# Causal mask added on VectorE together with the row maximum; opening transfers merged and cut smaller; the first norm's ones product one unit later

## The chip, the cores and the metric

The kernel runs on one core of one Trainium2 chip. The metric is device time in microseconds of one execution: three executions of the kernel before took 1414.01, 1414.11 and 1414.16 us, median 1414.11. The profiled execution is a further one, with its own time. Engines are named as in the profile: PE is TensorE's matmul, PEld its weight load, DVE is VectorE, ACT is ScalarE, POOL is GpSimd, SP is SyncE (which only issues transfers here; SPq and ACTq are the issuing instructions of two DMA queues).

## The reference

A decoder trunk of two layers over 528 tokens (16 learned meta tokens and 512 real ones), width 1024, all float32. Layer 0 mixes with an mLSTM group (4 heads, chunked) and an RG-LRU group; layer 1 with differential attention, 8 heads of two 64-wide query/key halves each; each layer is followed by a squared-ReLU MLP, with an RMS norm ahead of every part. What the change touches is the first norm and projection of layer 0, and the softmax of layer 1:

```python
h = x*rsqrt(mean(x*x)+eps)*g ; proj = h @ w_in            # layer 0, first product of the program
...
s = einsum('bhcqd,bhckd->bhcqk', qb, kh)                  # layer 1, c = 0, 1
p = softmax(where(k_pos <= q_pos, s, -inf))
pd = p[:, :, 0] - lam * p[:, :, 1]
out = einsum('bhqk,bhkv->bhqv', pd, vh)
```

## The kernel before

Tokens lie along the free dimension (528 columns), features on the 128 partitions, so an activation of width 1024 is 8 tiles of 128x528. A float32 product is made of three passes with reduced-precision operands: each operand is split into a high part (ACT's cast) and a low part (DVE's subtraction, the helper at L162), and PE computes high*high, high*low and low*high. A weight "unit" is 128x1024: it feeds 8 blocks of 128 columns, so a unit on all 528 tokens is 8 x 3 x 2 = 48 matmuls of 264 columns (L425). SP loads each unit; ACT casts it (L240) and DVE subtracts (L162).

**The opening.** `OPENING` (L78) is the order of the first transfers: the halves A0, A1 of the first unit, B0, B1 of the second, the eight blocks x0 to x7 of the input, and `pk`, a packed table of 116 constants per partition with the norm's gains. Two of them (x0 and pk, marked *) go out on ACT's queue, the rest on SP's (L562 to L578). `norm_x` (L474) turns block k into its scaled high part (ACT, L480) and low part (DVE, L482); `ahead_of` splits the weight halves between them. `TURNS` (L79) is the order in which `two_units` (L430, matmuls at L439) takes blocks 0 to 7 of the two units A and B: 96 matmuls. Until the first data are there PE runs 16 matmuls on a tile of ones (`N_WARM`, L179). The scale of the norm, 1/sqrt(mean square), is applied later, to the products: ACT squares the eight blocks (L515), POOL adds them (L517), ACT and DVE split the sum, PE multiplies it with a matrix of ones (L531), and ACT and DVE form `rstd`.

**The order of work** of layer 0 is the table `PLAN` (L46): `q00 q02` are the two units of the opening, `S` the squares, `N` the ones product with what follows it, `q01 q03` two more units, `e` the gate unit, `c0` the first unit whose result is multiplied with `rstd`.

**The attention.** `attend(hd)` (L1120) computes the q, k and v units of one head; `attn_steps` gives the steps s0 to s3 (scores and softmax of one block of 128 queries), t0 to t3 (transposes of the probabilities), v, o and f (values, output product, norm). `SLOTS` (L31) says at which of six places between the matmuls of `attend` each step of the previous heads is put (a ' means one head further back), and the scheduler then merges them into one instruction order per engine. A score step (L1188) has per half c one or two spans of at most 400 columns, each in one of the four "ax" PSUM banks: two matmuls (L1203, L1205), and for the span that holds the diagonal a third one of an identity with a bfloat16 matrix that is -2^100 above the diagonal (L1202 or L1208; both operands lie in `keepb`). DVE takes the negated row maximum (L1210; with two spans one more operation, L1214), ACT computes exp(score - maximum) from PSUM with the row sum (L1217). Later L1226 and L1227 scale and subtract the two halves.

Of the kernel before, what the change touches and what calls it, by code (L numbers as in the profile page):

```python
# [30 lines left out]
SLOTS = ("t2' s0 t1'", '', "t3'", 's1', "o' t0 s2 v", "f' s3")  # L31
# [15 lines left out]
q00 q02 S q01 N q03 e c0 q04 A o0 G0 B g0 q12 m1 c1 K q05 q10 C G1 m1 p1 p1 g1 o1 p1 p1 R0 q11 m2  # L47
# [76 lines left out]
def trunk(tc, hT, wu, wri, pk, lv, rope, gf, out, probe=None):  # L124
# [7 lines left out]
    with ctx:  # L132
# [36 lines left out]
        keep = cp.tile([P, T], F32, name="keep")  # L169
        keepr = cp.tile([P, P], F32R, name="keepr")  # L170
        ones, ident, mkf, pkt = (keep[:, i * P:i * P + w] for i, w in enumerate((P, P, P, N_PK)))
        onesr = keepr[:, 0:P]
        keepb = cp.tile([P, 2 * P], mybir.dt.bfloat16, name="keepb")
        mkr, idr = (keepb[:, i * P:(i + 1) * P] for i in range(2))
        nc.vector.memset(onesr.bitcast(F32), 1.0)
        nc.vector.memset(ones, 1.0)
        warm = axt("warm")
        for _ in range(N_WARM):
            nc.tensor.matmul(warm[:, :2 * P], onesr, onesr[:, None, :].to_broadcast([P, 2, P]), start=True, stop=True)  # L179
        epsc = cp.tile([P, 1], F32, name="epsc")  # L180
# [293 lines left out]
        def norm_x(h, gc, lo, tag, late=False, hold=KB, then=None):  # L474

            x = [xt(f"{tag}x{k}") for k in range(KB)]
            fin = []
            for k in range(KB):
                hk = h[:, k, lo:]
                fin_x = nc.scalar.activation(out=x[k][0][:, lo:], in_=hk, func=AF.Copy, scale=pc(gc + k))  # L480
# [80 lines left out]
        last = {}  # L561
        for t in OPENING:  # L562
            if t == "##":
                with tc.issue_after(last[True].ins):
                    last[True] = nc.scalar.copy(cp.tile([P, 1], F32, name="first"), ones[:, 0:1])
                continue
            on = t.endswith("*")
            eng = nc.scalar if on else nc.sync
            with tc.issue_after(last[on].ins) if on in last else nullcontext():
                if t[:2] == "pk":  # L570
                    last[on] = eng.dma_start(out=pkt, in_=pk)
                elif t[0] == "x":
                    i = int(t[1])
                    last[on] = eng.dma_start(out=h0[:, i, :], in_=hT[:, i, :])
                else:
                    u, i = "AB".index(t[0]), int(t[1])
                    c = slice(i * HALF, (i + 1) * HALF)
                    last[on] = eng.dma_start(out=raws[u][:, c], in_=wu[seq[u]][:, c])  # L578

        c = slice(0, HALF)  # L580
        state["first"] = nc.vector.tensor_copy(out=ready[0][0][:, c], in_=raws[0][:, c])

        def ahead_of(k):
            seen = [t[:2] for t in OPENING if t[:2] not in ("pk", "##")]
            at = 0 if k == 0 and seen[0][0] != "x" else seen.index(f"x{k}") + 1
            while at < len(seen) and seen[at][0] != "x":
                u, i = "AB".index(seen[at][0]), int(seen[at][1:])
                c = slice(i * HALF, (i + 1) * HALF)
# [491 lines left out]
        for i in range(2):  # L1080
# [12 lines left out]
        nc.vector.memset(mkf, 0.0)  # L1093
        nc.gpsimd.affine_select(out=mkf, in_=mkf, pattern=[[-1, P]], compare_op=ALU.is_ge, fill=NEG, base=0,
                                channel_multiplier=1)
        nc.vector.tensor_copy(out=mkr, in_=mkf)
        nc.vector.tensor_copy(out=idr, in_=ident)
# [74 lines left out]
        def attn_steps(hd, rot, vr):  # L1172
# [15 lines left out]
            def sstep(I):  # L1188
# [5 lines left out]
                for c in range(2):  # L1194
# [4 lines left out]
                    for r, (d, s0, m) in list(enumerate(spans))[::-1 if c else 1]:  # L1199
                        masked = s0 + m == nk  # L1200
                        if c and masked:
                            nc.tensor.matmul(d[:, m - P:m], idr, mkr, start=True, stop=False, skip_group_check=True)  # L1202
                        nc.tensor.matmul(d[:, :m], qS[c][:, qs], kS[c][:, s0:s0 + m], start=not (c and masked),  # L1203
                                         stop=False, skip_group_check=True)
                        nc.tensor.matmul(d[:, :m], qS[c][:, qs], kL[c][:, s0:s0 + m], start=False,  # L1205
                                         stop=bool(c) or not masked, skip_group_check=True)
                        if not c and masked:
                            nc.tensor.matmul(d[:, m - P:m], idr, mkr, start=False, stop=True, skip_group_check=True)  # L1208
                        with pri("E"):
                            nc.vector.tensor_reduce(out=mx[:, 2 * c + r:2 * c + r + 1], in_=d[:, :m], axis=AX.X, op=ALU.max,  # L1210
                                                    negate=True)
                    with pri("E"):
                        if len(spans) == 2:
                            nc.vector.tensor_tensor(out=mx[:, 2 * c:2 * c + 1], in0=mx[:, 2 * c:2 * c + 1],  # L1214
                                                    in1=mx[:, 2 * c + 1:2 * c + 2], op=ALU.min)
                        for r, (d, s0, m) in enumerate(spans):
                            nc.scalar.activation(out=e[:, s0:s0 + m], in_=d[:, :m], func=AF.Exp,  # L1217
                                                 bias=mx[:, 2 * c:2 * c + 1], accum_out=ss[:, c + 2 * r:c + 2 * r + 1])
# [154 lines left out]
def lay_out(x, meta_tokens, norm_mix, norm_mlp, norm_final, ab_w_in, ab_if_bias, mlstm_norm, lru_conv_w, lru_conv_b,  # L1373
# [81 lines left out]
    return {"hT": hT, "wu": wu.reshape(N_UNIT, P, 1024), "wri": wri, "pk": pk, "lv": lv, "rope": rope,  # L1455
# [18 lines left out]
```

## Time and profile before

| what | value |
|---|---|
| time, median of 3 (range) | 1414.11 us (1414.01 to 1414.16) |
| time of the profiled execution | 1414.54 us |
| its span, first to last instruction | 1412.7 us |
| PE busy | 1399.7 us, 99% |
| DVE / ACT / POOL busy | 72% / 54% / 13% |
| mean clock granted to PE | 0.998 |

How to read it: an engine's busy time is counted in the span; what lies between the span and the time (1.8 us here) is start and end. Matmuls overlap in the record (each is shown from its start to its modelled end), so the price of one in a row of them is the distance to the next start, not its duration. A group of instructions is shown as line, engine, operation, output<-inputs, shape and count, then busy time, mean ns of one, and the idle time ahead of it with what ended it.

### The profile page before, as it was taken

What the parts mean: (1) busy time and instruction counts of PE and PEld (TensorE: products, weight loads), DVE (VectorE), ACT (ScalarE), POOL (GpSimd) and SP (SyncE); (2) the same over time, 40 slices, a digit from 0 to 9 for tenths busy, and PEclk for the clock granted to TensorE, in tenths of its full rate; (3) what the DMA queues carried; (4) which work ended last, traced back from release to release, by engine and by line L of the source; (5) the groups of instructions that cost most, each with busy time, mean ns of one, the idle gap of its engine ahead of it and who ended that gap; (6) DMA issues with size and microseconds to landing.
All of it is one profiled execution on the core that took longest, in us unless ns stands there. A gap on an engine that the chain in (4) does not pass through costs nothing.

```text
span 1412.7 us, 25718 instructions
## 1 busy us (share of the span) xinstructions
PE 1399.7 (99%) x10258; PEld 1329.5 (94%) x10258; DVE 1015.3 (72%) x1787; ACT 764.7 (54%) x1345; POOL 180.3 (13%) x268
## 2 busy tenths in 40 slices
PE   8999999999999999999999999999999999999998
PEld 8999999999999999999999999999887899899986
DVE  5867663756845998888886467878778977777752
ACT  6465743747434555656554335666656454454542
POOL 3000001010003024444430300000002000000001
PEclk9999999999999999999999999999999999999999
DMA  7342324223134369899972266565442332233231
GB/s 245 106 107 86 93 67 127 74 76 104 60 90 135 100 225 359 299 317 309 306 265 88 108 217 196 167 187 158 158 149 75 134 120 96 84 119 105 75 119 45
DMA packets 69924, 210.18 MB, mean 149 GB/s; under 512 B 12682, under 2 KB 14231, under 8 KB 69804
## 3 DMA queue, kind: packets, MB, share of 16 engines
q1 hardware_dynamic: 52300, 154.65, 34.3%
q0 software_dynamic: 15360, 50.34, 9.6%
q10 hardware_dynamic: 2144, 3.54, 0.8%
q8 instruction: 80, 1.31, 0.4%
q14 instruction: 40, 0.33, 0.1%
HBM read 162.11 MB, written 35.71 MB: 140 GB/s over the span
## 4 chain that ended last, share of the span: by engine, by line
PE 95%; ACT 2%; DVE 1%; DMA 1%; POOL 1%; issue 0%; SPq 0%; POOLq 0%; ACTq 0%
PE mm L425 34%; PE mw L988 23%; PE mpY L344 8%; PE mpX L344 5%; PE mpZ L344 5%; PE mn L988 4%; PE mo L1302 3%; PE mf L1338 3%; PE po L1262 1%; PE pnum L712 1%; PE pt L1238 1%; PE pss L688 1%; PE mm L439 1%; PE psc L1203 1%; PE psc L1205 1%; POOL nsq L517 1%
## 5 line engine op out<-in xcount | busy, mean ns | idle before, releaser
L240 ACT CAST wh<-raw 128x1024 fp32r<-128x1024 f32 x139 | 145.3, 1048 | 268.6 <-PE mm L425 79.8
L988 PE MATMUL mw<-al,wh 128*128 128x264 f32 (+1 forms) x704 | 221.2, 314 | 0.0
L988 PE MATMUL mw<-ah,wl 128*128 128x264 f32 (+1 forms) x704 | 221.1, 314 | 0.0
L988 PE MATMUL mw<-ah,wh 128*128 128x264 f32 (+1 forms) x704 | 221.1, 314 | 0.0
L162 DVE TENSOR_TENSOR wl<-raw,wh 128x1024 fp32r<-128x1024 f32 (+1 forms) x136 | 164.3, 1209 | 58.1 <-ACT wh L240 55.7
L988 PEld LDWEIGHTS mw<-ah,wl 128*128 128x128 f32 x704 | 132.5, 188 | 8.3
L988 PEld LDWEIGHTS mw<-al,wh 128*128 128x128 f32 x704 | 132.4, 188 | 7.4
L988 PEld LDWEIGHTS mw<-ah,wh 128*128 128x128 f32 x704 | 132.4, 188 | 7.4
L1032 DVE TENSOR_TENSOR h<-mw,h 128x264 f32<-128x264 f32 (+1 forms) x176 | 87.5, 497 | 22.0 <-PE mw L988 21.3
L517 POOL TENSOR_TENSOR nsq<-nsq 128x528 f32<-128x528 f32 (+1 forms) x28 | 43.2, 1542 | 362.5 <-ACT nsq L515 361.7
L344 PE MATMUL mpX<-xp,A_h 128*128 128x264 f32 (+1 forms) x416 | 77.2, 282 | 0.0
L344 PEld LDWEIGHTS mpX<-xp,A_h 128*128 128x128 f32 x416 | 65.0, 188 | 1.0
L344 PE MATMUL mpX<-xp,A_l 128*128 128x264 f32 (+1 forms) x208 | 58.8, 283 | 0.0
L162 DVE TENSOR_TENSOR al<-rt,ah 128x528 fp32r<-128x528 f32 (+1 forms) x64 | 46.1, 720 | 17.7 <-ACT ah L165 16.7
L1210 DVE TENSOR_REDUCE mx<-psc 128x1 f32<-128x264 f32 (+3 forms) x80 | 33.2, 433 | 21.6 <-PE psc L1205 11.5
L279 ACT CAST S_h<-sums 128x1024 fp32r<-128x1024 f32 x26 | 27.3, 1050 | 37.1 <-issue 12.5
L1351 POOL TENSOR_TENSOR zg<-z,gfr 128x512 f32<-128x512 f32 x4 | 5.2, 1292 | 328.3 <-DVE z L1345 317.6
L998 ACT ACTIVATE rt<-rt 128x528 f32<-128x528 f32 (+1 forms) x64 | 40.7, 638 | 9.9 <-DVE rt L1019 8.8
L1217 ACT ACTIVATE e<-psc,mx 128x264 f32<-128x264 f32 (+3 forms) x80 | 38.1, 481 | 13.1 <-DVE mx L1210 7.6
L162 DVE TENSOR_TENSOR ral<-ra,rah 128x512 fp32r<-128x512 f32 x64 | 43.7, 683 | 1.7 <-DMA ra<-wu 0.5
L1250 ACT CAST pp<-pt 128x128 fp32r<-128x128 f32 (+2 forms) x64 | 21.1, 343 | 40.2 <-PE pt L1238 35.7
L165 ACT CAST ah<-rt 128x528 fp32r<-128x528 f32 (+1 forms) x64 | 40.1, 627 | 1.5
(940 smaller groups left out, 4409.3 us busy)
## 6 DMA issues: line engine op xcount, KB each, us to landing
raw<-wu SPq DMA_DIRECT2D x139, 512.0 KB
rawp<-wu SPq DMA_DIRECT2D x26, 1024.0 KB
ra<-wu POOLq DMA_DIRECT2D x64, 256.0 KB, 5.7
h<-hT SPq DMA_DIRECT2D x15, 264.0 KB
st<-rh SPq DMA_DIRECT2D x16, 132.0 KB
st<-rh ACTq DMA_DIRECT2D x16, 132.0 KB
kz<-rl SPq DMA_DIRECT2D x16, 132.0 KB
st<-rh SPq DMA_DIRECT2D x16, 128.0 KB
```

What stands on the lines that cost most here:

```text
L162: eng.tensor_tensor(out=o, in0=a, in1=b, op=ALU.subtract)
L165: nc.scalar.copy(hl[0][:, sl], src)
L240: nc.scalar.copy(wh, raw)
L344: nc.tensor.matmul(st[b][:, :hv], ww[:, cc], xx, start=st[b, "n"] == 0, stop=k == 3 and j == 2, skip_group_check=True)
L425: nc.tensor.matmul(p[:, :m], w[:, c], xx[:, s:s + m], start=(k == 0 and j == 0), stop=(k == KB - 1 and j == len(terms) - 1))
L517: state["kz"] = nc.gpsimd.tensor_tensor(out=fin[0][:, lo:], in0=fin[0][:, lo:], in1=sq[:, lo:], op=ALU.add)
L988: nc.tensor.matmul(ps, w[ww], x[xx][:, tk], start=k == j == 0, stop=k == len(ws) - 1 and j == 2)
L998: nc.scalar.activation(out=t[:, cols], in_=t[:, cols], func=AF.Square)
L1032: nc.vector.tensor_tensor(out=hf, in0=ps, in1=hf, op=ALU.add)
L1217: nc.scalar.activation(out=e[:, s0:s0 + m], in_=d[:, :m], func=AF.Exp, bias=mx[:, 2 * c:2 * c + 1], accum_out=ss[:, c + 2 * r:c + 2 * r + 1])
L1302: nc.tensor.matmul(ps, w[ww][:, b], co[k][xx][:, NM:], start=(k == ks[0] and j == 0), stop=(k == ks[-1] and j == 2))
L1338: nc.tensor.matmul(pss[n][:, :m], a[k][aa][:, tk], w[k][ww][:, f0:f0 + m], start=(k == 0 and i == 0), stop=(k == KB - 1 and i == 2))
```

## The change

Four things are joined.

1. The mask. The identity-times-mask matmuls are gone. The mask is one bfloat16 tile `mkw` of 400 columns, zero but for its last 128. For a span with the diagonal DVE runs one fused operation (`tensor_tensor_reduce`) in the place of the maximum: it adds scores and mask, negates, writes the result to SBUF (`e`) and takes the row minimum of it; where there are two spans, the minimum starts from that of the first, so the extra minimum is gone. On the engine it is two instructions, the operation and one that stores the accumulated minimum. ACT's exponential of that span then reads `e` from SBUF (with scale -1), not the scores from PSUM. `SLOTS` puts the steps of a head at other places.
2. The opening. The constants and block x0 lie side by side in memory and come in one transfer, 644 columns wide. All opening transfers go out on SP's queue; the two units are cut into pieces of 256, 256 and 512 columns, A and B in turn.
3. `N` stands one unit later in `PLAN`, behind `q03`.
4. 17 warming matmuls, not 16. The copy of the constants to their later place is a POOL instruction.

```diff
-SLOTS = ("t2' s0 t1'", '', "t3'", 's1', "o' t0 s2 v", "f' s3")
+SLOTS = ("t2' s0", '', "t1' t3'", '', "o' s2", "v f' s3 t0 s1")
...
-q00 q02 S q01 N q03 e c0 q04 A o0 G0 B g0 q12 m1 c1 K q05 q10 C G1 m1 p1 p1 g1 o1 p1 p1 R0 q11 m2
+q00 q02 S q01 q03 N e c0 q04 A o0 G0 B g0 q12 m1 c1 K q05 q10 C G1 m1 p1 p1 g1 o1 p1 p1 R0 q11 m2
...
-N_WARM = 16
-OPENING = "A0 x0* pk* ## x1 A1 x2 B0 x3 B1 x4 x5 x6 x7".split()
-TURNS = "A0 A1 A2 B0 A3 B1 B2 A4 B3 A5 B4 A6 B5 A7 B6 B7".split()
-HALF = 512
+N_WARM = 17
+OPENING = "A0 x0 B0 x1 A1 x2 B1 x3 A2 x4 B2 x5 x6 x7".split()
+TURNS = "A0 B0 A1 B1 A2 B2 A3 B3 A4 B4 A5 B5 A6 B6 A7 B7".split()
+PIECES = (slice(0, 256), slice(256, 512), slice(512, 1024))
...
+        hp = big.tile([P, 2 * T], F32, tag="hp", name="hp", bufs=1)
+        state["h0"], state["x0"], pk0 = h0, hp[:, T:], hp[:, T - N_PK:T]
...
+            if t == "x0":
+                nc.sync.dma_start(out=hp[:, T - N_PK:], in_=pk)
...
+        nc.gpsimd.tensor_copy(out=pkt, in_=pk0)
...
-                    for r, (d, s0, m) in list(enumerate(spans))[::-1 if c else 1]:
-                        masked = s0 + m == nk
-                        if c and masked:
-                            nc.tensor.matmul(d[:, m - P:m], idr, mkr, start=True, stop=False, skip_group_check=True)
...
-                        if not c and masked:
-                            nc.tensor.matmul(d[:, m - P:m], idr, mkr, start=False, stop=True, skip_group_check=True)
...
+                    top = float(3.0e38)
+                    for r, (d, s0, m) in enumerate(spans):
+                        nc.tensor.matmul(d[:, :m], qS[c][:, qs], kS[c][:, s0:s0 + m], start=True, stop=False)
+                        nc.tensor.matmul(d[:, :m], qS[c][:, qs], kL[c][:, s0:s0 + m], start=False, stop=True)
+                        a = mx[:, 2 * c + r:2 * c + r + 1]
                         with pri("E"):
...
+                            if s0 + m == nk:
+                                nc.vector.tensor_tensor_reduce(out=e[:, s0:nk], in0=d[:, :m], in1=mkw[:, 400 - m:], scale=-1.0,
+                                                               scalar=top, op0=ALU.add, op1=ALU.min, accum_out=a)
+                            else:
+                                nc.vector.tensor_reduce(out=a, in_=d[:, :m], axis=AX.X, op=ALU.max, negate=True)
+                        top = a
...
+                            nc.scalar.activation(out=e[:, s0:s0 + m], in_=e[:, s0:nk] if last else d[:, :m], func=AF.Exp,
+                                                 scale=-1.0 if last else 1.0, bias=top,
+                                                 accum_out=ss[:, c + 2 * r:c + 2 * r + 1])
```

Outside the opening and the attention the order of PE's instructions is the one of before. Three places matter. First, the opening on SP's queue (`raw` are the two units, `h` the input blocks, `hp` the joined transfer). Before:

```order
L578 DMA raw_164<-wu 128x512
L574 DMA h_163<-hT 128x528
L578 DMA raw_164<-wu 128x512
L574 DMA h_163<-hT 128x528
L578 DMA raw_165<-wu 128x512
L574 DMA h_163<-hT 128x528
L578 DMA raw_165<-wu 128x512
L574 DMA h_163<-hT 128x528 x4
```

And now:

```order
L575 DMA raw_168<-wu 128x256
L570 DMA hp<-pk 128x644
L575 DMA raw_169<-wu 128x256
L572 DMA h_166<-hT 128x528 x2
L575 DMA raw_168<-wu 128x256
L572 DMA h_166<-hT 128x528
L575 DMA raw_169<-wu 128x256
L575 DMA raw_168<-wu 128x512
L572 DMA h_166<-hT 128x528
L575 DMA raw_169<-wu 128x512
L572 DMA h_166<-hT 128x528 x3
```

The joined transfer is SP's second; before, block x0 and the constants were the only two transfers on ACT's queue, in that order.

Second, PE behind the unit q01 (`mm_391`, `mm_392` and `mm_399`, `mm_400` are its two PSUM banks, `nps` the ones product). Before:

```order
L425 MATMUL mm_391<-ax7h,wl_242 128x264
L425 MATMUL mm_392<-ax7h,wl_242 128x264
L531 MATMUL nps<-nsh,keepr 128x264
L531 MATMUL nps<-nsl,keepr 128x264
L531 MATMUL nps<-nsh,keepr 128x264
L531 MATMUL nps<-nsl,keepr 128x264
L425 MATMUL mm_473<-ax0h,wh_247 128x264
```

And now:

```order
L426 MATMUL mm_399<-ax7h,wl_250 128x264
L426 MATMUL mm_400<-ax7h,wl_250 128x264
L426 MATMUL mm_461<-ax0h,wh_255 128x264
L426 MATMUL mm_462<-ax0h,wh_255 128x264
L426 MATMUL mm_461<-ax0l,wh_255 128x264
L426 MATMUL mm_462<-ax0l,wh_255 128x264
```

The 48 matmuls of the next unit, q03, now stand between q01 and the ones product.

Third, PE in the attention, in a middle head (`psc` are scores, `pt` transposes, `keepb` the mask's operands). Before, a score step of 272 columns stood after all transposes of another block:

```order
L1238 MATMUL pt<-keep,e_11963 72x128 x2
L1238 MATMUL pt<-keep,e_11963 128x128 x3
L1203 MATMUL psc<-st_11842,st_11733 128x272
L1205 MATMUL psc<-kz_10423,st_11733 128x272
L1208 LDWEIGHTS keepb
L1208 MATMUL psc<-keepb 128x128
L1202 LDWEIGHTS keepb
L1202 MATMUL psc<-keepb 128x128
L1203 MATMUL psc<-st_11843,st_11734 128x272
L1205 MATMUL psc<-kz_10424,st_11734 128x272
L425 MATMUL mm_12120<-dx6h,wl_11916 128x264
```

And now, in the q unit of the next head:

```order
L1199 MATMUL psc<-st_11441,st_11345 128x264
L1200 MATMUL psc<-kz_10427,st_11345 128x264
L426 MATMUL mm_12016<-dx3h,wh_11725 128x512
L1234 MATMUL pt<-keep,e_11642 72x128 x2
L426 MATMUL mm_12016<-dx3l,wh_11725 128x512
L426 MATMUL mm_12016<-dx3h,wl_11726 128x512
L1199 MATMUL psc<-st_11440,st_11344 128x272
L1200 MATMUL psc<-kz_10426,st_11344 128x272
L426 MATMUL mm_12016<-dx4h,wh_11725 128x512
L1199 MATMUL psc<-st_11441,st_11345 128x272
L1200 MATMUL psc<-kz_10427,st_11345 128x272
L426 MATMUL mm_12016<-dx4l,wh_11725 128x512
```

The mask's four rows are gone, and the steps s3 (264 columns), t0, s1 (272 columns) and behind them s0 of the next head follow each other with one or two matmuls of the q unit in between.

More of the change, by code (lines that the diff above doesn't have):

```diff
@@ L166, in split @@
             sub(eng or nc.vector, hl[1][:, sl], src, hl[0][:, sl].bitcast(F32))
-        keep = cp.tile([P, T], F32, name="keep")
+        keep = cp.tile([P, 2 * P + 200 + N_PK], F32, name="keep")
         keepr = cp.tile([P, P], F32R, name="keepr")
-        ones, ident, mkf, pkt = (keep[:, i * P:i * P + w] for i, w in enumerate((P, P, P, N_PK)))
+        ones, ident, pkt = keep[:, :P], keep[:, P:2 * P], keep[:, 2 * P + 200:]
+        mkw = keep[:, 2 * P:2 * P + 200].bitcast(mybir.dt.bfloat16)
         onesr = keepr[:, 0:P]
-        keepb = cp.tile([P, 2 * P], mybir.dt.bfloat16, name="keepb")
-        mkr, idr = (keepb[:, i * P:(i + 1) * P] for i in range(2))
         nc.vector.memset(onesr.bitcast(F32), 1.0)
         nc.vector.memset(ones, 1.0)
+        nc.scalar.copy(cp.tile([P, 1], F32, name="first"), ones[:, 0:1])
         warm = axt("warm")
@@ L479, in norm_x @@
                 hk = h[:, k, lo:]
-                fin_x = nc.scalar.activation(out=x[k][0][:, lo:], in_=hk, func=AF.Copy, scale=pc(gc + k))
+                hk = state["x0"][:, lo:] if late and not k else hk
+                gk = pk0[:, gc + k:gc + k + 1] if late else pc(gc + k)
+                fin_x = nc.scalar.activation(out=x[k][0][:, lo:], in_=hk, func=AF.Copy, scale=gk)
                 with tc.issue_after(state["first"].ins) if then and not k else nullcontext():
-                    nc.vector.scalar_tensor_tensor(out=x[k][1][:, lo:], in0=hk, scalar=pc(gc + k),
+                    nc.vector.scalar_tensor_tensor(out=x[k][1][:, lo:], in0=hk, scalar=gk,
                                                    in1=x[k][0][:, lo:].bitcast(F32), op0=ALU.mult, op1=ALU.subtract)
@@ L514, in norm_sq @@
             sq = sc("nsq")
-            nc.scalar.activation(out=sq[:, lo:], in_=h[:, k, lo:], func=AF.Square)
+            hk = state["x0"] if h is state["h0"] and not k else h[:, k, lo:]
+            nc.scalar.activation(out=sq[:, lo:], in_=hk, func=AF.Square)
             if k:
@@ L560, in trunk @@
         state["next"] = 2
-        last = {}
         for t in OPENING:
[L563 to L580, printed above, removed]
+            i = int(t[1:])
+            if t == "x0":
+                nc.sync.dma_start(out=hp[:, T - N_PK:], in_=pk)
+            elif t[0] == "x":
+                nc.sync.dma_start(out=h0[:, i, :], in_=hT[:, i, :])
+            else:
+                u, c = "AB".index(t[0]), PIECES[i]
+                nc.sync.dma_start(out=raws[u][:, c], in_=wu[seq[u]][:, c])
+        c = PIECES[0]
         state["first"] = nc.vector.tensor_copy(out=ready[0][0][:, c], in_=raws[0][:, c])
         def ahead_of(k):
[L584 to L588, printed above, removed]
+            at = OPENING.index(f"x{k}")
+            todo_ = OPENING[:at] if k == 0 else []
+            for t in OPENING[at + 1:]:
+                if t[0] == "x":
+                    break
+                todo_ = todo_ + [t]
+            for t in todo_:
+                u, i = "AB".index(t[0]), int(t[1:])
+                c = PIECES[i]
                 (wh, wl), raw = ready[u], raws[u]
@@ L1091, in trunk @@
         nc.vector.tensor_copy(out=lam, in_=psl[:, 0:1])
[L1093 to L1097, printed above, removed]
+        nc.gpsimd.affine_select(out=mkw[:, 272:], in_=mkw[:, 272:], pattern=[[-1, P]], compare_op=ALU.is_ge, fill=NEG,
+                                base=0, channel_multiplier=1)
         gsub = cp.tile([P, 1], F32, name="gsub")
@@ L1454, in lay_out @@
         rope[1, o:o + 8], rope[1, o + 8:o + 16] = -sin.T, sin.T
-    return {"hT": hT, "wu": wu.reshape(N_UNIT, P, 1024), "wri": wri, "pk": pk, "lv": lv, "rope": rope,
+    return {"hT": hT, "wu": wu.reshape(N_UNIT, P, 1024), "wri": wri, "pk": np.concatenate([pk, hT[:, 0]], axis=1), "lv": lv, "rope": rope,
             "gf": np.ascontiguousarray(norm_final.reshape(1, 1024))}
```

15 lines of the change are left out of this document (3 added, 12 removed).

## The prediction

> **What bounds the kernel now.** I read the page first (busy time), then PE's list of waits, then windows of stages, then the order of time in the places that the change touches.
>
> ```profile
> span 1412.7 us, 25718 instructions
> PE 1399.7 (99%) x10258; PEld 1329.5 (94%) x10258; DVE 1015.3 (72%) x1787; ACT 764.7 (54%) x1345; POOL 180.3 (13%) x268
> ```
>
> PE is busy for all but 13.0 us, so only two things shorten the program: fewer or denser matmuls, and PE's few waits. The list of what PE waited for (us in total, times, longest) names them:
>
> ```profile
> PE mm L439 <- ACT ax0h L480: 2.1, 1, 2.1
> ...
> PE psc L1202 <- ACT e L1217: 0.7, 1, 0.7
> ...
> PE nps L531 <- DVE lm L162: 0.4, 1, 0.4
> ```
>
> The first is the wait for the first block of data, the second is the only visible one in the attention, at a mask matmul, the third is ahead of the ones product. The change is aimed at all three. Four windows (length, then busy time and count of PE, PEld, DVE, ACT, POOL, then granted clock, DMA share, GB/s):
>
> ```profile
> 4.17:7.58 3.41, 1.26 (x9) 0.84 (x7) 2.10 (x5) 1.59 (x3) 0.00 (x0) 1.00 1.01 356
> 7.58:10.99 3.41, 3.41 (x16) 3.41 (x17) 3.41 (x7) 3.31 (x6) 0.00 (x0) 0.53 1.05 400
> ...
> 20.31:40.00 19.69, 19.22 (x156) 18.81 (x155) 10.88 (x20) 12.60 (x24) 7.68 (x5) 1.00 0.68 217
> 891.50:1020.70 129.20, 129.20 (x890) 116.87 (x888) 102.10 (x274) 81.76 (x231) 0.00 (x0) 1.00 0.56 175
> ```
>
> After a stretch with PE busy for 1.26 of 3.41 us its clock is half for the next 3.41 us, in the middle of real work. Around the ones product 0.47 us are idle (19.69 - 19.22). In five heads of the attention PE is never idle; DVE is busy for 79%, ACT for 63%.
>
> **The opening.** In order of time (start, duration, instruction; the first row is from the chain of waits):
>
> ```profile
> 0.73 4.09 DMA h<-hT
> ```
>
> ```profile
> 1.19 0.45 ACTq L571 DMA_DIRECT2D keep<-pk  x1
> ...
> 5.99 0.73 ACT L480 ACTIVATE ax0h<-h,keep 128x528 fp32r<-128x528 f32 x1 [2.83 <-DMA keep<-pk]
> ```
>
> ```profile
> 1.05 3.62 PE L179 MATMUL warm<-keepr 128*128 128x256 f32 x16 [1.05 <-DVE keepr L175]
> 6.78 0.51 PE L439 MATMUL mm<-ax0h,wh 128*128 128x264 f32 x2 [2.10 <-ACT ax0h L480]
> ...
> 20.43 0.28 PE L425 MATMUL mm<-ax0h,wh 128*128 128x264 f32 x1
> ```
>
> Block x0 lands at 4.82, but the constants only at 5.97, and ACT waits for the later one; PE starts 0.79 behind ACT. Now both come together, 322 KB behind a first weight piece of 128 KB, 450 KB in place of the 520 KB (x0 and half of A) that had landed at 4.82, though issued second on SP, some 0.4 later. Earliest: 450/520 of 4.09 behind 0.73, or 4.3; latest 5.97, as the constants did. I take 4.8, near x0's row: PE starts at 5.6 (5.1 to 6.8) instead of 6.78, **-1.2**.
>
> From 6.78 to 20.43 the 96 matmuls take 13.65 us. At full clock one takes 0.12 (rows 969.84 and 969.96 below), 96 take 11.6. Of the 2.0 lost, the slow window explains 16 x (3.41/16 - 0.12) = 1.5, early waits the other 0.5. With 17 warming matmuls (0.11 more, inside the wait: free; its cover is PE's idle time until 5.6) PE works to 4.8 and from 5.6 to 7.58, so it is busy for 2.6 of the 3.41 us that were busy for 1.26. I take it that the clock then stays up: **-1.5** (or 0). The other 0.5 I leave. ACT can feed this: 8 activations and 5 casts of at most 0.73 end at 14.3, and block 7 is needed by PE at 5.6 + 7 x 1.46 = 15.8. Sum of the opening -2.7, bounds +0.0 and -3.6.
>
> [...]
>
> **The ones product** (ends of q01, start of the product's second half, start of q03, and `rstd` on DVE):
>
> ```profile
> 26.03 0.41 PE L425 MATMUL mm<-ax7h,wl 128*128 128x264 f32 x2
> ...
> 27.29 0.39 PE L531 MATMUL nps<-nsl,keepr 128*128 128x264 f32 x1 [0.35 <-DVE lm L162]
> ...
> 27.76 0.41 PE L425 MATMUL mm<-ax0h,wh 128*128 128x264 f32 x2
> ```
>
> ```profile
> 32.23 0.71 DVE L471 SCALAR_TENSOR_TENSOR arstd<-rqa,rqy 128x528 f32<-128x528 f32 x1
> ```
>
> Its inputs are ready at 27.3, set by POOL's additions, not by PE. With PE 2.7 early and q03 (48 x 0.12 = 5.8) ahead, PE comes to it at 26.3 - 2.7 + 5.8 = 29.4: the idle **-0.5** goes, and the opening's gain is not given back here. Without the move it would be, 2.7 lost: it is the cover of the opening. What gets later is `rstd`: 5.0 behind the product's start before (32.94), so about 35 now. Its first user on PE's path is the evacuation of c0, 32 + 48 matmuls or 9.6 us behind the product, at 39: hidden by 4 us.
>
> **The mask matmuls.** Eight heads, four blocks, two halves: 64 go. A pair of score groups of 400 columns in PE's order of time:
>
> ```profile
> 968.85 0.43 PE L1203 MATMUL psc<-st,st 128*128 128x400 f32 x1
> 969.12 0.34 PE L1205 MATMUL psc<-kz,st 128*128 128x400 f32 x1
> 969.30 0.23 PE L1208 MATMUL psc<-keepb 128*128 128x128 bf16 x1
> 969.36 0.22 PE L1202 MATMUL psc<-keepb 128*128 128x128 bf16 x1
> 969.39 0.43 PE L1203 MATMUL psc<-st,st 128*128 128x400 f32 x1
> 969.66 0.34 PE L1205 MATMUL psc<-kz,st 128*128 128x400 f32 x1
> 969.84 0.28 PE L425 MATMUL mm<-dx2h,wh 128*128 128x264 f32 x1
> 969.96 0.41 PE L425 MATMUL mm<-dx2l,wh 128*128 128x264 f32 x2
> ```
>
> Without the two, the second L1203 starts at 969.30 with its weights loaded, and two distances of 0.18 bring the next row to 969.66, not 969.84: 0.18 a pair, 32 pairs, **-5.8**. Lower bound: the two masks' own distances alone, 0.06 + 0.03, 2.9. Upper bound: PEld's idle time at these lines comes on top, 5.8 + 3.2 = 9.0:
>
> ```profile
> PEld L1202 <- issue: 1.8, 7, 0.3
> PEld L1208 <- issue: 1.4, 8, 0.2
> ```
>
> **What DVE and ACT take over.** Groups (count, busy us, mean ns):
>
> ```profile
> L1210 DVE TENSOR_REDUCE mx<-psc 128x1 f32<-128x400 f32 x16 | 8.6, 569 | 2.0 <-PE psc L1208 1.7 <-PE psc L1205 0.2
> ...
> L1210 DVE TENSOR_REDUCE mx<-psc 128x1 f32<-128x144 f32 x16 | 4.8, 298 | 5.4 <-PE psc L1208 5.4
> ...
> L1214 DVE TENSOR_TENSOR mx<-mx 128x1 f32<-128x1 f32 x16 | 2.4, 153 | 0.3
> ```
>
> ```profile
> L1345 DVE TENSOR_TENSOR z<-mf,ht 128x256 f32<-128x256 f32 x2 | 0.8, 424 | 3.8 <-PE mf L1338 3.8
> ...
> L1347 DVE SCALAR_TENSOR_TENSOR zq<-z 128x256 f32<-128x256 f32 x1 | 0.4, 424 | 0.0
> ...
> L1347 DVE DVE_READ_ACCUMULATOR zq<-z 128x1 f32 x1 | 0.1, 80 | 0.0
> ```
>
> ```profile
> L1217 ACT ACTIVATE e<-psc,mx 128x400 f32<-128x400 f32 x16 | 9.3, 588 | 0.5 <-PE mm L425 0.5
> ```
>
> ```profile
> L1226 ACT ACTIVATE e<-e,rs 128x400 f32<-128x400 f32 x8 | 5.0, 630 | 0.3 <-DVE rs L1225 0.2
> ```
>
> The trace has no fused operation with a PSUM operand. Its two nearest rows agree: a reduction takes 1.06 ns a column (271/256), 417 ns at 256 columns, and an addition from PSUM (L1345) or an accumulating operation (L1347) of 256 takes 424. So it costs what the reduction did, plus the accumulator's 0.08: 64 x 0.08 - 16 x 0.153 = +2.7 us of DVE, hidden in its idle fifth (2.7 on the path if not). ACT reads SBUF: 630 against 588, 64 x 0.04 = +2.7, hidden in its idle third. In return a masked span's PSUM bank is free after DVE, not after ACT.
>
> **The moved steps.** s1 and t0 now stand with s3, v and the next head's s0 in one burst; of the bank users there, a score waits until DVE or ACT has emptied an earlier bank, and the q unit's matmuls are queued behind it on PE. Per head at best nothing (and the visible 0.7 goes), at worst about two such operations, 1.0. Nearer to nothing, since before PE shows no idle there: half an operation every other time, 0.2 a head, **+1.6** (-0.7 to +8).
>
> **Sum**: -2.7 - 0.5 - 5.8 + 1.6 = -7.4. The profiled execution took 1414.54, span 1412.7, so its successor would have a span of 1405.3 and a time of 1407.1; the median lies 0.43 lower: **1406.7**.
>
> **Rivals.**
> - *The opening gains little* (clock slow again from 7.58, or the joined transfer as late as the constants were): +1.5 to +2.7, 1408.2 to 1409.4. For it: 1.26 busy of 3.41 was too little, and nothing shows how much is enough. Against: 2.6 is twice that. 17%.
> - *The burst eats the masks' gain*: 1.0 us of bank waits per head, 8 in place of 1.6, 1413.1. For it: the steps stand one or two matmuls (0.23 each) apart, and one fused operation needs 0.5. Against: the banks are freed earlier. 12%.
> - *The fused operation runs at half rate*, slower than before: 1.06 ns more a column, in the burst of a head 2 x (264 + 272 + 144) = 1360 columns, 1.44 us, 11.5 in eight heads if PE waits for all of it: 1406.7 + 11.5 = 1418.2. Waits above 9.0 / 8 = 1.1 us a head make it slower. Against: L1347 with two operands takes what L1345 takes. 7%. [...]
> - *PE's weight waits go with the masks*: 3.2 more, 1403.5. 10%.
>
> **The numbers.** The forecast has 54%, its own range 1404.5 to 1408. A measurement of this kernel tells 0.2%, 2.8 us, from no change: faster is below 1411.3, slower above 1416.9. Faster: 54 + 17 + 10 and a quarter of the second rival, 84%; same 9%; slower 7%. Range 1402.8 to 1411.8: it leaves out half rate and most of the burst rival.
>
> **What would show it.** First L439 row at 5.6 and granted clock 1.00 from 7.58 to 10.99; the first matmul of q01 near 17.7; no PE idle ahead of L535; two score groups of 400 columns 0.81 from first row to the next unit's matmul, not 0.99; the fused operation at 400 columns near 0.57 with 0.08 behind it; PE waits at L1199 below 2 us. The forecast is wrong if PE waits there for DVE or ACT by more than 4 us, or the fused operation is above 0.8.

## The result, and the profile after

| | before | changed |
|---|---|---|
| time, median of 5 (range) | 1414.11 us (1413.67 to 1414.54) | 1405.64 us (1405.32 to 1406.45) |
| time / span of the profiled execution | 1414.54 / 1412.7 us | 1405.64 / 1403.8 us |

The ratio is 0.994 (95% interval 0.9929 to 0.9952): 8.5 us faster, where 7.4 were forecast. The page of the changed kernel begins:

```profile
span 1403.8 us, 25656 instructions
PE 1393.8 (99%) x10195; PEld 1324.9 (94%) x10195; DVE 1012.8 (72%) x1834; ACT 766.3 (55%) x1347; POOL 179.3 (13%) x270
```

PE's busy time fell by 5.9 us, its idle time from 13.0 to 10.0. PE's list of waits in the changed kernel (us in total, times, longest):

```profile
PE warm L179 <- DVE keepr L174: 1.1, 1, 1.1
PE mm L426 <- ACT yb6h L165: 0.8, 1, 0.8
PE pss L689 <- DVE vl L671: 0.5, 1, 0.5
PE mm L440 <- DVE wl L162: 0.3, 1, 0.3
PE mm L440 <- ACT ax1h L483: 0.3, 1, 0.3
PE mm L440 <- ACT ax0h L483: 0.2, 1, 0.2
```

The 2.1 us in front of the first data are 0.2; the ones product (now L535) and the scores (L1199, L1200) are not in the list any more. The same windows as before the change (length, busy time and count of PE, PEld, DVE, ACT, POOL, then granted clock, DMA share, GB/s):

```profile
4.17:7.58 3.41, 2.89 (x20) 2.43 (x19) 1.71 (x3) 1.63 (x3) 0.17 (x1) 1.00 0.96 280
7.58:10.99 3.41, 3.07 (x22) 2.61 (x21) 2.64 (x7) 3.19 (x6) 0.00 (x0) 1.00 1.00 373
...
20.31:40.00 19.69, 19.69 (x164) 19.69 (x164) 12.92 (x22) 13.72 (x26) 9.14 (x6) 1.00 0.67 215
```

No half clock from 7.58 on, and no idle time around the ones product. In order of time, the opening of the changed kernel (start, duration, instruction, idle time ahead and what ended it):

```profile
4.04 0.74 ACT L483 ACTIVATE ax0h<-hp 128x528 fp32r<-128x528 f32 x1 [1.82 <-DMA hp<-pk]
...
4.83 0.51 PE L440 MATMUL mm<-ax0h,wh 128*128 128x264 f32 x2 [0.24 <-ACT ax0h L483]
...
6.21 0.74 ACT L483 ACTIVATE ax1h<-h,hp 128x528 fp32r<-128x528 f32 x1 [1.14 <-DMA h<-hT]
...
18.30 0.29 PE L426 MATMUL mm<-ax0h,wh 128*128 128x264 f32 x1
```

PE has data 1.95 us earlier (4.83 for 6.78), then waits for the next block, which ACT gets only at 6.21; q01 begins at 18.30, 2.1 us earlier than before. A pair of score groups of 400 columns in the changed kernel:

```profile
933.43 0.40 PE L1199 MATMUL psc<-st,st 128*128 128x400 f32 x1
933.66 0.34 PE L1200 MATMUL psc<-kz,st 128*128 128x400 f32 x1
933.84 0.34 PE L1199 MATMUL psc<-st,st 128*128 128x400 f32 x1
934.02 0.35 PE L1200 MATMUL psc<-kz,st 128*128 128x400 f32 x1
934.21 0.41 PE L426 MATMUL mm<-dx0h,wh 128*128 128x264 f32 x2
```

From its first row to the next unit's row it takes 0.78 us, where it took 0.99. The groups on DVE and ACT that took over (count, busy us, mean ns, idle time ahead; the operation and the row that stores its minimum):

```profile
L1204 DVE CUSTOM_DVE_ANT_0 e<-psc,keep 128x400 f32<-128x400 f32 x16 | 8.5, 569 | 0.0
L1204 DVE CUSTOM_DVE_ANT_0 e<-psc,keep,mx 128x264 f32<-128x264 f32 x16 | 7.8, 485 | 0.3 <-PE psc L1200 0.3
...
L1204 DVE DVE_READ_ACCUMULATOR2_ANT mx<- 128x1 f32 x64 | 5.2, 82 | 0.0
```

```profile
L1212 ACT ACTIVATE e<-e,mx 128x400 f32<-128x400 f32 x16 | 9.9, 622 | 6.2 <-DVE mx L1204 6.2
```

Where the time went is seen by laying PE's rows of the two executions side by side. The changed kernel is ahead by 2.1 us at the start of q01, by 3.2 at 41 us (behind the ones product), by 4.0 at 101, by 4.0 at 825 (with up to 4.9 between, which comes back), and by 9.05 at the first MLP row behind the attention (1060.1), 8.9 at the end. The attention gave 5.0 us, what lies ahead of it 4.0.

### The profile page after: what moved, and what is told of

The parts are those of the page before. It is cut to its first block, busy times and chain, and to the rows that moved or that the text cites. A ratio compares the mean times of both kernels' runs of the same rounds, so it can differ in the third digit from the quotient of the medians.

```text
span 1403.8 us, 25656 instructions
## 1 busy us (share of the span) xinstructions
PE 1393.8 (99%) x10195; PEld 1324.9 (94%) x10195; DVE 1012.8 (72%) x1834; ACT 766.3 (55%) x1347; POOL 179.3 (13%) x270
## 4 chain that ended last, share of the span: by engine, by line
PE 90%; DVE 3%; DMA 2%; ACT 2%; issue 1%; POOL 1%; SPq 0%; ACTq 0%; POOLq 0%; DVEq 0%
PE mm L426 30%; PE mw L989 23%; PE mpY L345 8%; PE mpZ L345 5%; PE mpX L345 5%; PE mn L989 4%; PE mo L1298 3%; PE mf L1334 3%; PE po L1258 2%; PE pnum L713 1%; DMA raw<-wu 1%; PE mm L440 1%; PE pt L1234 1%; PE psc L1199 1%; PE pss L689 1%
## 5 line engine op out<-in xcount | busy, mean ns | idle before, releaser
L1033 DVE TENSOR_TENSOR h<-mw,h 128x264 f32<-128x264 f32 (+1 forms) x176 | 87.6, 498 | 23.0 <-PE mw L989 21.8
L280 ACT CAST S_h<-sums 128x1024 fp32r<-128x1024 f32 x26 | 27.3, 1052 | 39.1 <-issue 12.5
L165 ACT CAST rah<-ra 128x512 fp32r<-128x512 f32 x64 | 37.8, 613 | 5.7 <-DMA ra<-wu 5.6
L352 DVE TENSOR_TENSOR hh<-mpZ,hh 128x264 f32<-128x264 f32 (+1 forms) x52 | 22.2, 426 | 25.9 <-PE mpZ L345 25.8
L1212 ACT ACTIVATE e<-e,mx 128x144 f32<-128x144 f32 (+3 forms) x64 | 32.8, 514 | 13.6 <-DVE mx L1204 13.3
```

Of the source, the lines that this page charges most:

```text
L165: nc.scalar.copy(hl[0][:, sl], src)
L1033: nc.vector.tensor_tensor(out=hf, in0=ps, in1=hf, op=ALU.add)
L1212: nc.scalar.activation(out=e[:, s0:s0 + m], in_=e[:, s0:nk] if last else d[:, :m], func=AF.Exp, scale=-1.0 if last else 1.0, bias=top, acc ...
```

## The experiments

Times are medians of 4 to 11 executions; the kernel before, measured again beside them, stands at 1413.97 to 1414.37 us.

| run | time, us | ratio to before (95%) |
|---|---|---|
| mask and new places alone | 1409.45 | 0.9968 (0.9955 to 0.9980) |
| mask, old places | 1409.66 | 0.9970 (0.9961 to 0.9979) |
| opening and ones product alone | 1409.93 | 0.9972 (0.9960 to 0.9984) |
| opening, ones product at its old place | 1416.21 | 1.0015 (1.0006 to 1.0025) |
| no mask, old places | 1409.05 | 0.9964 (0.9951 to 0.9977) |
| ones product alone moved | 1413.27 | 0.9997 (0.9987 to 1.0006) |
| the same, 26 warming matmuls | 1412.31 | 0.9988 (0.9978 to 0.9998) |
| changed, fused operation twice | 1447.91 | 1.0243 (1.0228 to 1.0258) |
| changed, joined transfer, halves | 1409.72 | 0.9966 (0.9954 to 0.9979) |
| no mask, new places | 1411.96 | 0.9986 (0.9977 to 0.9995) |
| changed, s1 out of the burst | 1406.29 | 0.9945 (0.9932 to 0.9957) |
| changed, 8 warming matmuls | 1406.52 | 0.9944 (0.9931 to 0.9956) |

### The mask, with the new and the old places of the steps

To the kernel before, the fused operation and its tile `mkw` are added as in the change, first with the new `SLOTS`, then with the old:

```diff
-SLOTS = ("t2' s0 t1'", '', "t3'", 's1', "o' t0 s2 v", "f' s3")
+SLOTS = ("t2' s0", '', "t1' t3'", '', "o' s2", "v f' s3 t0 s1")
```

> The kernel before with the mask on VectorE and the new places of the steps; opening, ones product and warming matmuls as before. Theory (read off where the two traces drift apart: PE's rows shift by -4.0 us ahead of the attention and by -9.0 behind it): the attention alone gives 5.0 of the 8.5, so 1409.1 us (1408.6 to 1409.7), and the rows ahead of the attention stand where they stood before, within 0.3 us. Rival, by the sum of the prediction (-5.8 for the masks, +1.6 for the burst): 1409.9. Rival two, the parts need each other (the attention's gain is larger or smaller with the old opening): outside 1408.5 to 1410.5.

> As the run with the mask alone, but with the steps of a head at their old places. Theory of the prediction: the moved steps cost 1.6 us (2.0 by the traces, where the matmuls around the transposes and output products became slower by that much), so without them the mask gives 7.0: 1407.1 us, 2 less than the mask with the new places. Rival: the new places are what makes room for the fused operation; with the old ones PE waits for VectorE or ScalarE at the scores, by 1 to 3 us, and the time is 1410 to 1412.

1409.45 and 1409.66 us. The mask with the new places gives 4.8, near the 5.0 read off the traces. The new places make no difference that can be measured: neither the 2 us that the first theory wanted back nor the loss of the second.

### The same two places without any mask

The lines of the mask matmuls are taken out of the kernel before, and nothing is put in their place, so these two kernels leave the masking out; the second has the new `SLOTS` as well.

```diff
-                        if c and masked:
-                            nc.tensor.matmul(d[:, m - P:m], idr, mkr, start=True, stop=False, skip_group_check=True)
...
-                        if not c and masked:
-                            nc.tensor.matmul(d[:, m - P:m], idr, mkr, start=False, stop=True, skip_group_check=True)
```

> The kernel before without its 64 mask matmuls and with nothing in their place: the masking is left out, all else stays, the steps at their old places. Theory one (from the run of the mask with the old steps, where the scores' rows became 4.4 us shorter in all): with these places of the steps the masks are worth 4.4, the fused operation costs PE nothing, 1409.8 us (1409.3 to 1410.3). Theory two (the prediction's price of 0.18 a pair, or the 6.7 by which the scores' rows became shorter with the new places): they are worth 5.8 to 6.7 anywhere, 1408.4 to 1407.5, and the mask with the old steps lost 1.2 to 2.1 of it to the fused operation.

> The kernel before without mask matmuls (the masking is left out, nothing in its place), and with the steps at their new places. It stands to the run without masks at the old places (1409.05) as the mask with the new places stands to the mask with the old ones (1409.45 and 1409.66). Theory one: what the new places give back (1.2 us at the transposes and output products) comes from the places and not from the fused operation, and is balanced by denser scores: 1409.0 (1408.6 to 1409.5). Theory two: it comes from the fused operation's longer way through VectorE, so that here only the denser scores (2.3 us) remain: 1406.8 (1406.4 to 1407.5).

1409.05 and 1411.96 us. At the old places the masks are worth 4.9 us, between the two theories, and the fused operation, which does the masking, stands 0.6 above that: nearly all of it is hidden. At the new places, however, the kernel without masks loses 2.9 us, against both theories, and is 2.5 slower than the kernel that does the masking with the fused operation there. The time from each PE row's start to the next one's, added up between the last unit ahead of the attention and the MLP behind it (us, one profiled execution of each), shows where:

| PE rows | before | changed | mask, new places | mask, old places | no mask, old | no mask, new |
|---|---|---|---|---|---|---|
| 64 mask matmuls | 3.92 | 0 | 0 | 0 | 0 | 0 |
| 160 scores | 25.03 | 21.99 | 22.26 | 24.58 | 24.38 | 25.19 |
| - of these 32 of 144 columns (s0) | 4.05 | 3.48 | 3.72 | 5.29 | 5.40 | 6.98 |
| 112 transposes | 9.77 | 10.35 | 10.36 | 9.58 | 9.86 | 10.26 |
| 120 output products | 20.54 | 21.09 | 21.14 | 20.82 | 20.73 | 21.34 |
| all the rest | 171.34 | 172.13 | 172.22 | 171.60 | 170.81 | 171.24 |
| sum | 230.6 | 225.6 | 226.0 | 226.6 | 225.8 | 228.0 |

The new places cost 1.0 to 1.1 us at the transposes and output products, mask or none. With the fused operation they win that back at the scores, and s0 above all, which stands last in the burst, is dense: 3.48 in the changed kernel, 3.72 with the mask alone. With the mask alone the scores are 2.3 shorter at the new places than at the old, but 1.15 of that are two waits at s0 in the execution with the old places, 0.82 for a transfer into `kz` and 0.33 for DVE's `vr`, which none of the other five has; it took 1410.77 us, 1.1 above its median. Without the fused operation s0 at the new places takes 6.98. What it waits for stands in PE's own list of waits of that kernel, and its row of groups says that all of it is at the spans of 144 columns, s0:

```profile
PE psc L1200 <- ACT e L1210: 1.0, 5, 0.2
```

```profile
L1200 PE MATMUL psc<-st,st 128*128 128x144 f32 x16 | 5.0, 315 | 1.2 <-ACT e L1210 1.0
```

PEld's list of that kernel has the same wait (first), and so has PEld's list of the changed kernel (second), where PE itself has none of it:

```profile
PEld psc L1200 <- ACT e L1210: 2.2, 7, 0.4
```

```profile
PEld psc L1199 <- ACT e L1212: 1.5, 5, 0.4
```

In the kernel without masks it is ACT's exponential that holds the bank. With the fused operation a masked span's bank is free after DVE, since ACT reads SBUF: that is what pays for the new places, and only there.

### The opening, with and without the move of the ones product

The first run is the change without its mask part (mask on PE, old `SLOTS`); the second differs by

```diff
-q00 q02 S q01 q03 N e c0
+q00 q02 S q01 N q03 e c0
```

> The kernel before with the new opening, 17 warming matmuls and the ones product one unit later; the mask stays on PE, the steps at their old places. Theory: -2.1 for the opening, -1.0 at the ones product, -0.7 at a wait for cb in the first mixer, as the drift of PE's rows shows: 1410.2 us. Rival, by the prediction's terms (-2.7 and -0.5): 1410.9; rival two, the 0.7 at cb is chance and not tied to the opening: 1411.0. The first matmul of q01 at 18.3 in all of them.

> As the run with the opening alone, but with the ones product at its old place, ahead of q03. Theory of the prediction (the later place is the cover of the opening): the inputs of the product come from POOL's additions, not from PE, so PE, 2.1 us early, waits for them at about 24.2 until 27 or later; the whole gain is given back: 1413.5 to 1415 us, with 2.5 us or more of waiting at the ones product. Rival: the additions move forward with the opening, and the product gives back 0.5 at most: 1411.7.

1409.93 and 1416.21 us. The opening with the move gives 4.3; without the move it is 2 us slower than before the change. The move is worth 6.3 us there, because without it PE waits at the ones product. The first rows of the product at its old place, and ACT's row that it waits for:

```profile
28.65 0.39 PE L536 MATMUL nps<-nsh,keepr 128*128 128x264 f32 x1 [3.51 <-ACT nsh L165]
29.39 0.39 PE L536 MATMUL nps<-nsl,keepr 128*128 128x264 f32 x1 [0.35 <-DVE nsl L162]
```

```profile
27.96 0.63 ACT L165 CAST nsh<-nsq 128x528 fp32r<-128x528 f32 x1 [2.05 <-POOL nsq L522]
```

In the kernel before, ACT's row stood at 25.86, in the changed kernel at 28.12 (ACT's rows in order of time, one fence each):

```profile
25.86 0.63 ACT L165 CAST nsh<-nsq 128x528 fp32r<-128x528 f32 x1 [0.68 <-POOL nsq L517]
```

```profile
28.12 0.63 ACT L165 CAST nsh<-nsq 128x528 fp32r<-128x528 f32 x1 [2.10 <-POOL nsq L521]
```

So the new opening makes the sum of squares 2.3 us later, not earlier. POOL's additions, 1.4 to 1.6 us each, set it. Before, six of ACT's eight squares were done when it turned to the cast at 19.15, and POOL had six additions in a row; now only three are done, and the others stand behind a weight cast that itself waits 2.14 us for its transfer. POOL is idle for 2.42 us until they come. The changed kernel's rows, ACT's cast and POOL's last five additions, then POOL's row before:

```profile
18.74 1.05 ACT L241 CAST wh<-raw 128x1024 fp32r<-128x1024 f32 x1 [2.14 <-DMA raw<-wu]
```

```profile
21.03 7.05 POOL L521 TENSOR_TENSOR nsq<-nsq 128x528 f32<-128x528 f32 x5 [2.42 <-ACT nsq L519]
```

```profile
16.42 9.41 POOL L517 TENSOR_TENSOR nsq<-nsq 128x528 f32<-128x528 f32 x6 [0.76 <-ACT nsq L515]
```

With the product at its old place the wait costs once more: of 3.41 us from 26.68 on PE works 1.09, and the next 3.41 run at half clock.

```profile
26.68:30.09 3.41, 1.09 (x6) 0.89 (x7) 2.35 (x5) 2.13 (x5) 1.25 (x1) 1.00 0.65 193
30.10:33.51 3.41, 3.41 (x18) 3.41 (x17) 0.52 (x2) 3.32 (x6) 2.38 (x1) 0.50 0.77 278
```

### The ones product and the clock, each by itself

The kernel before with the ones product moved as in the change; then also with `N_WARM = 26`.

> The kernel before with one edit, the ones product behind q03. Prediction: the visible idle time of 0.47 us goes, 1413.7. By the distances of PE's starts there (26.03 to 27.76, of which the last two q01 matmuls and the four of the product need 0.73): 1.0 goes, 1413.2. Rival: the scale comes later by 5.9 us and is waited for at c0: no gain or a loss, 1414.2 or more.

> The same with 26 warming matmuls instead of 16, which fill PE until about 6.5 us, 0.3 short of the first data; the transfers are those of before. Theory of the prediction (PE's busy share from 4.17 to 7.58 decides on the clock from 7.58 to 10.99): granted clock 1.00 there in place of 0.53, and 1.5 us less than the run with the ones product alone moved: 1411.7. Rival one: the clock comes back, but PE then waits for blocks from ScalarE and VectorE, and less than 0.5 is left. Rival two: the low clock does not come from the idle time, and stays: no difference.

1413.27 us: PE's rows behind the product are 1.03 us earlier, as the distances of starts say, twice the visible idle time (the difference in the medians is too small to be told from none). With 26 warming matmuls 1412.31, another 1.0. The windows of PE's first data in that run:

```profile
4.17:7.58 3.41, 2.56 (x19) 2.15 (x17) 2.13 (x5) 1.62 (x3) 0.00 (x0) 1.00 1.05 377
7.58:10.99 3.41, 3.18 (x23) 2.91 (x24) 3.41 (x7) 3.41 (x7) 0.00 (x0) 1.00 1.05 402
```

The half clock is gone, so filling PE's idle time does keep the clock up; but 0.23 us of PE's second stretch are idle again, and q01 starts at 19.48 instead of 20.38: 0.9, not 1.5. PE then waits for blocks instead, so the first rival has a part in it too.

### Joined, but in halves; and fewer warming matmuls

Two edits of the changed kernel, each alone:

```diff
-OPENING = "A0 x0 B0 x1 A1 x2 B1 x3 A2 x4 B2 x5 x6 x7".split()
-TURNS = "A0 B0 A1 B1 A2 B2 A3 B3 A4 B4 A5 B5 A6 B6 A7 B7".split()
-PIECES = (slice(0, 256), slice(256, 512), slice(512, 1024))
+OPENING = "A0 x0 x1 A1 x2 B0 x3 B1 x4 x5 x6 x7".split()
+TURNS = "A0 A1 A2 B0 A3 B1 B2 A4 B3 A5 B4 A6 B5 A7 B6 B7".split()
+PIECES = (slice(0, 512), slice(512, 1024))
```

```diff
-N_WARM = 17
+N_WARM = 8
```

> The changed kernel with the constants and block x0 still joined and on SP's queue, but the first two units in halves of 512 columns, in the order of before (x0, x1, A1, x2, B0 behind A0; the order of the blocks as before). Theory (the cutting sets the start): 578 KB must land ahead of the first matmul, not 450, some 0.4 us more at the 318 GB/s of that stretch, so PE starts at 5.3, not 4.83, and has only one block of work until x1 is there; q01 0.4 to 0.9 later than 18.30, 1406.0 to 1406.5 us. Rival: the larger rows move faster (375 to 400 GB/s in the kernel before against 250 to 300 with pieces), x1 comes earlier and nothing is lost: 1405.2 to 1405.7. Rival two: the joining does it all, and PE starts at 4.8.

> The changed kernel with 8 warming matmuls instead of 17: they end near 2.7 us, PE is idle until 4.83, 2.1 us as it was in the kernel before between its warming matmuls and the data. Theory (PE's busy time in one stretch of 3.41 us sets the clock of the next: in the run with the doubled fused operation stretches with 1.69, 1.82 and 1.89 us were followed by 0.50 to 0.52, those with 1.95 and more by 1.00): here 0.76 to 4.17 has 1.7 us busy, so granted clock near 0.5 from 4.17 to 7.58, q01 1.0 to 1.5 us later than 18.30, 1406.6 to 1407.1 us. Rival (gaps of that length leave the clock up): clock 1.00, 1405.6 us.

Halves: 1409.72 us, 4.1 more than the changed kernel, far beyond the 0.4 to 0.9 of the first theory. PE's first data matmul is at 5.45, 0.6 later, but then PE has nothing for 1.35 us (block x2 reaches ACT at 8.65, not 7.74), and that idle time brings the half clock back. The granted clock of its second and third stretch:

```profile
6.64:10.05 3.41, 2.01 (x14) 1.56 (x12) 2.09 (x3) 2.05 (x5) 0.00 (x0) 1.00 1.03 355
10.06:13.47 3.41, 3.41 (x17) 3.41 (x16) 3.41 (x7) 3.36 (x6) 0.00 (x0) 0.50 1.04 350
```

q01 starts at 21.39, later than before the change. With 2.01 us busy the first of these stretches lies where the clock went either way (see below), so not every execution need fall. Still, all five (1408.30 to 1410.61) are slower than the slowest of the changed kernel (1406.45), and their median is not below that of the mask alone (1409.45): in halves the joined transfer gains nothing that can be measured. Whether the smaller pieces or the turns of A and B do it was not separated. The profiled execution is 4.8 longer than the changed kernel's; 3.1 of it stand at q01 and another 0.9 between 41 and 101 us, with a wait of 0.8 for `cb` that the changed kernel does not have. The rest is not explained.

8 warming matmuls: 1406.52 us, 0.9 more, with ranges that overlap (1405.26 to 1407.28 against 1405.32 to 1406.45). In the profiled execution, in which q01 starts at 19.03, 0.7 later, the first data are at 5.26 (the transfer landed 0.44 later), and the windows show something else than expected:

```profile
6.29:9.70 3.41, 3.41 (x17) 3.41 (x17) 2.44 (x5) 2.80 (x5) 0.00 (x0) 1.00 1.02 339
9.70:13.11 3.41, 3.41 (x30) 3.41 (x30) 3.17 (x7) 3.21 (x5) 0.00 (x0) 1.00 0.94 315
```

Both are full of matmuls of 264 columns, 17 in one and 30 in the other, though the clock column reads 1.00 in both. The column shows only changes, and the first one recorded is the rise at 9.70: until then the clock is low. So neither theory had it right, though the first came near the time: the clock did not fall at 4.17, it had not risen yet.

### The fused operation twice, and one step out of the burst

```diff
+                                for _ in range(2):
                                     nc.vector.tensor_tensor_reduce(out=e[:, s0:nk], in0=d[:, :m], in1=mkw[:, 400 - m:], scale=-1.0,
```

```diff
-SLOTS = ("t2' s0", '', "t1' t3'", '', "o' s2", "v f' s3 t0 s1")
+SLOTS = ("t2' s0", '', "t1' t3'", 's1', "o' s2", "v f' s3 t0")
```

> The changed kernel with each fused operation done twice in a row, the same result both times: 64 x (0.45 + 0.08) = some 34 us more work for VectorE in the attention, 79% busy becoming 93%; it is what an operation at half rate would have cost. Rival of the prediction (PE waits for all of it in the burst): +11.5, 1417.1 us. Theory: most of it is hidden, since the bursts are 16 us apart and PE's weight loads wait only 1.7 us in all for ScalarE or VectorE at the scores now; +1 to +4, 1406.6 to 1409.6.

> The changed kernel with one step moved: s1 back to its old place, out of the burst of v, f, s3, t0 and the next head's s0. Theory one (the burst of five is tight, as the doubled fused operation showed with 42 us): PE's weight loads no longer wait for ScalarE at the scores (1.5 us) and output products (1.3 us), 1404.4 us (1403.8 to 1405.0). Theory two (what a step gains by standing in the burst, its weights loaded behind another step's, it loses here): 1405.6 within 0.6.

Twice: 1447.91 us, 42 more for 34 us of added operations (the durations of their rows; DVE's busy time grows by 23, since rows overlap). Both expectations fall; nothing of it is hidden. Nor is it the price of half rate, as was expected: by the prediction's 1.06 ns a column, half rate would add some 18 us to the 64 operations (an estimate), not 34. The page of this run and PE's first waits:

```profile
PE 1414.4 (98%) x10195; PEld 1341.1 (93%) x10195; DVE 1036.0 (72%) x1962; ACT 769.8 (53%) x1347; POOL 178.8 (12%) x270
```

```profile
PE psc L1199 <- DVE mx L1205: 15.6, 15, 1.5
PE mo L1299 <- ACT co7h L165: 4.2, 1, 4.2
```

Idle time of PE grew from 10.0 to 31.8 us, and its busy time by 20.6, because the waits bring the half clock back: from 860 to 1100 us the granted clock is 0.92 in the mean. Two places of that run, each a stretch and the next ones:

```profile
873.56:876.97 3.41, 0.93 (x4) 0.45 (x4) 3.36 (x12) 1.91 (x7) 0.00 (x0) 1.00 0.00 0
876.97:880.38 3.41, 3.35 (x13) 2.67 (x13) 3.15 (x13) 2.14 (x9) 0.00 (x0) 0.50 0.00 0
935.00:938.41 3.41, 2.19 (x17) 1.76 (x16) 3.14 (x9) 2.18 (x6) 0.00 (x0) 1.00 0.40 162
938.41:941.82 3.41, 1.79 (x10) 1.05 (x10) 3.41 (x12) 2.52 (x9) 0.00 (x0) 1.00 0.00 0
941.83:945.24 3.41, 3.23 (x15) 3.23 (x15) 3.41 (x19) 2.63 (x10) 0.00 (x0) 0.50 0.01 2
```

In the two stretches in which PE has least to do (0.93 and 1.79 us) DVE is busy for 3.36 and 3.41 of 3.41 us: the mean share of 79% that it had before does not tell how full it is in the bursts. With s1 out of the burst 1406.29 us, not to be told from the changed kernel: the second theory, to 0.1 us. What the output products and transposes win (1.0 us) the scores and the units around s1 lose. None of these versions beats the changed kernel.

## Why the prediction was right, step by step

**The bound.** Right: PE alone sets the end. Additive too: the two halves of the change give 4.8 and 4.3, together 9.1, and the change 8.5, within the scatter of the medians.

**The opening, -2.7.** It was 2.1 in the profiled pair. The start of q01 differs from execution to execution: with the transfers of before 20.43, 20.42, 21.12, 21.64, 20.38 and 20.00, mean 20.67; with the new ones and 17 warming matmuls 18.30, 17.70, 19.16, 17.79 and 17.63, mean 18.12. That is -2.55, the size foretold, but by other parts whose errors cancel, which is luck. *The landing*: the first data matmul moved from 6.83 to 5.10 in the mean, -1.7 for the -1.2; the joined transfer reached ACT at 4.04 to 4.78, and the earliest bound of 4.3 was broken. It was scaled from a transfer time in which DMA was slow to start (128 GB/s from 2 to 3 us; 269 in the changed kernel). *The clock*: -0.8 between first data and q01 for the -1.5. Where it was measured alone it gave 0.9: the term took back all that the slow window costs, but PE is short of data there. In the changed kernel the clock is up from 3.9 us on, as the prediction had it.

**The clock's stretch.** Its length is on record: in the kernel before the clock is low from 7.754 to 11.167, 3.41 us. That a stretch with little work sets the next one's clock held wherever the stretches were counted from the changes of the clock on record (in the kernel before, with the ones product at its old place, with the fused operation twice and in halves): at full clock 0.92 to 1.79 us busy of 3.41 were always followed by half, 2.08 and more by full clock; between 1.86 and 2.01 both occur. That the stretches lie at 4.17 and 7.58 in every execution was wrong. By the counts of matmuls and the first change on record the clock rose at 3.9 us in the changed kernel, near 4.3 in the kernel before, at 9.7 in the run with 8 warming matmuls and at 13.25 in one without masks. Short waits were enough: in the kernel before one wait of 2.10 us lay ahead of the half clock, and in the run with the fused operation twice no wait in the scores was longer than 1.5 us, and the clock still fell, to 0.50 from 876.97 to 880.38.

**The ones product, -0.5.** -1.0 by PE's rows, in the changed kernel and with the move alone. What was mis-sized is the gain read from idle time: matmul ends are modelled, and the distances of starts (26.03 to 27.76, with six matmuls of 0.12 in it) held 1.0. **The cover.** That the move covers the opening was right, and its price too low: 6.3 measured, where the prediction's terms make 3.2 (the 2.7 that would be lost and the 0.5), since "its inputs are ready at 27.3" was taken over from the old opening. Of the 6.3 some 5.4 are the waits of 3.51 and 0.35 and what the half clock takes (18 matmuls in a stretch that holds 30 at full clock, 0.12 us each, an estimate). In the changed kernel the inputs are ready near 29.5, and PE arrives at 29.96: the margin is 0.5 us, not 2.1. The scale `rstd` is done at 37.67, not about 35, and PE still does not wait for it.

**The masks, -5.8, and the moved steps, +1.6.** Together -4.2; measured -4.8 alone and -5.0 in the trace. One part of the price was right: the pair of 400 columns takes 0.78 (0.81 foretold). Masks and scores together are 7.0 us shorter in the changed kernel, 1.2 more than the 5.8. But the steps were priced as if the places and the fused operation were independent: with the fused operation the new places cost -0.2, which is nothing that can be measured, without it +2.9. And the masks by themselves are worth 4.9 at the old places, not 5.8, so the two errors partly cancel. The sentence on the bank that becomes free after DVE named the reason and put no number to it.

**DVE and ACT.** The sizes were right: 569 ns and 82 ns for 0.57 and 0.08 at 400 columns, 622 for ACT's 630. One shape was not: 264 columns with a minimum from memory take 485, the plain reduction takes 431. Hidden, as foretold: 0.6 between the mask at the old places and no mask. **The rival of half rate** did not come true. Its price of 11.5 was probably too low, but no run has half rate: the doubled operation, nearly twice that work, cost 42. The price counted only the burst's own columns once, not the banks that stay full and not the clock that falls behind such waits.

**The sum.** -7.4 was forecast, -8.5 measured: 0.5 more at the ones product and 0.6 to 0.8 more in the attention. The wait of 0.7 for `cb` that PE had in the mixer before, and not in the changed kernel, lies between 0.2 and 0.8 in all other runs but one, which like the changed kernel shows none. The runs with it have either opening and either mask, so it looks like chance. Why PE's rows drift by 0.9 us and back between 101 and 825 us was not tried.

## What to carry to other kernels

When an opening gets faster, follow every input of the next waiting point through the new order, since the engine that prepares it may have become later: here a move worth 1.0 by itself was worth 6.3 with the new opening. Before calling work on another engine hidden, double it once: a mean share of 79% covered the work as it was and not twice that. Price a wait of PE by the distances between starts, and read its clock from the count of matmuls in a full window (17 against 30 here) as well as from the clock column.

## What was not expected of the hardware

The clock of PE depends on stretches of 3.41 us whose place differs from execution to execution, so that the same opening costs up to 1.6 us more or less (q01 at 20.00 to 21.64 with the old transfers; in the second of these, without masks and with the steps at their old places, the clock was low for some 6.2 us behind the first data: 18 matmuls from 9.84 to 13.25, 30 in the next 3.41 us). In the run with the fused operation twice short waits cost double: 21.8 us more idle time came with 20.6 us more busy time. And two changes that look independent were not: the new places of the steps lost 2.9 us or nothing, depending on which engine empties the bank.
